# Priority for the emptying of banks in the pairs of the first matrix, and a pinned first step of each pair's weights

## The chip, the cores and the metric

The kernel runs on one core of one Trainium2 chip. The metric is the device time of one execution in microseconds (us); lower is better. Five engines work side by side, each through its own instructions in a fixed order: TensorE (PE in the rows, with its weight loads as PEld), VectorE (DVE), ScalarE (ACT), GpSimd (POOL) and SyncE (SP). The last two issue nearly all transfers here.

## The reference, cut to what matters

The model is a decoder trunk of two layers on 512 tokens of 1024 features in float32. Each layer has a mixer and then a feed-forward part, and it is the second that the change touches:

```
def sqrelu_mlp(x, w1, w2):
    return jnp.square(jax.nn.relu(x @ w1)) @ w2

x = layer_norm(DEEPNORM_ALPHA * x + sqrelu_mlp(x, ffn_w1[l], ffn_w2[l]), ...)
```

`ffn_w1` is 1024 x 4096 and `ffn_w2` is 4096 x 1024.

## The kernel before

Every float32 product is made from split operands. `split` (lines 116 to 118) rounds a tile to a high part on ScalarE (line 117) and subtracts it from the tile on VectorE to get the low part (line 118); three matmuls (high by high, high by low, low by high) then make one product. A weight arrives from HBM as a `raw` tile of 128 x 1024, over SyncE's queue; there are four such buffers, and the next load into one waits until the last step that reads it is done.

The feed-forward part of a layer works through the 4096 hidden features in four blocks of 1024. In each block the first matrix gives the hidden block `hb`, and `second` multiplies it with the second matrix. The hidden features of a block are eight units of 128; the first block does six of them plainly, and all other units are done two at a time by `pair`, with Strassen's scheme in Winograd's form: seven products instead of eight. So there are 13 pairs in a layer: one in block 0 and four in each of blocks 1, 2 and 3.

A pair has three PSUM banks, `ba`, `bb` and `bc`. Its seven products, twelve matmuls each, come in this order: b11 into `ba`; t1 into `bc`; t2 on top of b11 in `ba`; b21 into `bb`; t3 on top in `ba`; b22 on top in `bc`; t4 on top in `ba`. Between them the banks are read out: `p1` is copied from `ba` before t2 adds to it, `p5` from `bc` before b22, `u2` from `ba` before t3 (ScalarE, lines 903, 907 and 911); `c11`, `c22` and `c12` are added up on VectorE (line 826) after b21, t3 and b22. The add of `c22` reads `ba`, and so t4, which writes `ba` again, waits for it. After t4 come a ReLU of `c11` and `c12` together (line 925), of `c22` (927), of `c21` from `ba` (928) and two squares (839). In the last block each square is followed by splits into `hs` and `ho`.

The weights of a pair come from two raw tiles in five steps (`add_pair`): `first` splits one tile (for b11 and b21), `s1` adds the halves of the other tile and splits the sum (t1), `s2` (t2), `s3` (t3 and t4) and `s4` (b22) subtract and split. The steps of a pair are issued while the pair before it runs. In `second`, seven products of 24 matmuls each (line 955) follow; the first uses `o11`, a split of `hb` (`left`).

What sets the order is a scheduler: it takes the program's text, reckons with costs of its own when an instruction can run, and writes one fixed order for each engine. `urgent` runs a function with a raised priority (an offset of 300), so that its instructions, once they can run in the scheduler's reckoning, go ahead of others that stand earlier in the text. `tc.keep_in_program_order(i)` keeps an instruction behind everything that the text has above it on its engine.

Of the kernel before, what the change touches and what calls it, by code (L numbers as in the profile page):

```python
# [11 lines left out]
F32 = mybir.dt.float32  # L12
# [3 lines left out]
AF = mybir.ActivationFunctionType  # L16
ALU = mybir.AluOpType
# [30 lines left out]
def trunk(ctx, tc, a, out):  # L48
    nc = tc.nc
    V, A, G, PE = nc.vector, nc.scalar, nc.gpsimd, nc.tensor  # L50
# [9 lines left out]
    def bank(name="ps"):  # L60
        return psp.tile([P, 512], F32, tag="ps", name=name)
# [17 lines left out]
    def t2(name, shape=(P, 512), dt=F32):  # L79
        return pool["t"].tile(list(shape), dt, tag="t", name=name)  # L80
# [26 lines left out]
    got, ops, held = {}, deque(), deque()  # L107
# [7 lines left out]

    def split(h, l, src):
        A.activation(h, src, AF.Copy)  # L117
        V.tensor_tensor(l, src, h.bitcast(F32), op=ALU.subtract)  # L118

    def room(kind):  # L120
        n = 1 if kind == 1 else 2
# [15 lines left out]
    def ready():  # L137
        need, kind, fn = entries[W["ready"]]
        load_to(need)
        W["ready"] += 1  # L140
        c, h, l = take(kind)
        fn(h, l)
        ops.append((c, h, l))
        load_to(need + W["ahead"])
# [6 lines left out]
    def nxt():  # L151
        if not ops:
            ready()
        c, h, l = ops.popleft()
        held.append(c)
        return c, h, l

    def release(c):
        held.remove(c)
        W[c[0]] -= c[1]  # L160
# [6 lines left out]
    def add_load(dst, src):  # L167

        loads.append(lambda: nc.sync.dma_start(dst(), src))
        return len(loads)  # L170

    def raw(key):
        def dst():
            got[key] = rp.tile([P, 1024], F32, tag="raw", name="raw")
            return got[key]
        return dst
# [6 lines left out]
    def add_pair(u):  # L183

        add_load(raw(u), wst[u])
        k, st = add_load(raw(u + 1), wst[u + 1]), {}
        sub = lambda o, p, q: V.tensor_tensor(o, p, q, op=ALU.subtract)

        def first(h, l):
            split(h, l, got[u])  # L190

        def s1(h, l):
            a2, st["s"] = got[u + 1], t2("s")
            V.tensor_tensor(st["s"], a2[:, :512], a2[:, 512:], op=ALU.add)  # L194
            split(h, l, st["s"])

        def s2(h, l):
            sub(st["s"], st["s"], got[u][:, :512])
            split(h, l, st["s"])

        def s3(h, l):
            a1, a2 = got[u], got.pop(u + 1)
            sub(a2[:, :512], a1[:, :512], a2[:, :512])
            split(h, l, a2)

        def s4(h, l):
            a12 = got.pop(u)[:, 512:]
            sub(a12, a12, st.pop("s"))
            split(h, l, a12)

        return [(k, 2, first), (k, 1, s1), (k, 1, s2), (k, 2, s3), (k, 1, s4)]
# [83 lines left out]
    def urgent(fn):  # L295
        def go(*args, **kw):
            with tc.high_priority(offset=URGENT):
                return fn(*args, **kw)
        return go

    class Fill:
# [3 lines left out]
        def add(self, cost, fn):  # L305
            self.q.append((cost, fn))
# [516 lines left out]
    def ffn(layer, last, nfirst, c0, t_last):  # L823
        new_stage(u=8, h=7, t=4, p=6)
        W["un"] = 1
        add = lambda o, p, q: V.tensor_tensor(o, p, q, op=ALU.add)  # L826
        sub = lambda o, p, q: V.tensor_tensor(o, p, q, op=ALU.subtract)
        H, st = [None, None], {}
# [8 lines left out]
        def square(j, p):  # L837
            r = H[j][:, :, p, :]
            A.activation(r, r, AF.Square)
            if st["fin"]:  # L840
                for i in range(2):
                    h, l = st["hl"][j][i]
                    split(h[:, p, :], l[:, p, :], r[:, i, :])
# [39 lines left out]
        def pair(p, right):  # L883

            ba, bb, bc = (bank("pp")[:, :256] for _ in range(3))

            def prod(o, op, i, r, first):
                for k in range(4):
                    c = slice(512 * i + P * k, 512 * i + P * k + P)
                    w, z = (op[1][:, c], op[2][:, c]), right[r](k)  # L890
                    for n, (x_, y_) in enumerate(((0, 0), (0, 1), (1, 0))):
                        PE.matmul(o, w[x_], z[y_], start=first and k == n == 0, stop=k == 3 and n == 2,  # L892
                                  skip_group_check=True)

            def done(op):
                release(op[0])
                pump(2)

            p1, p5, u2 = t1("p1"), t1("p5"), t1("u2")
            c11, c12, c21, c22 = H[0][:, 0, p, :], H[0][:, 1, p, :], H[1][:, 0, p, :], H[1][:, 1, p, :]  # L900
            w = nxt()
            prod(ba, w, 0, "b11", True)
            A.activation(p1, ba, AF.Copy)
            v = nxt()
            prod(bc, v, 0, "t1", True)
            done(v)
            A.activation(p5, bc, AF.Copy)
            v = nxt()
            prod(ba, v, 0, "t2", False)
            done(v)  # L910
            A.activation(u2, ba, AF.Copy)
            prod(bb, w, 1, "b21", True)
            done(w)
            add(c11, p1, bb)
            w = nxt()
            prod(ba, w, 0, "t3", False)
            add(c22, p5, ba)
            v = nxt()
            prod(bc, v, 0, "b22", False)
            done(v)  # L920
            add(c12, u2, bc)
            prod(ba, w, 1, "t4", False)
            done(w)
            r = H[0][:, :, p, :]
            A.activation(r, r, AF.Relu)
            square(0, p)
            A.activation(c22, c22, AF.Relu)
            A.activation(c21, ba, AF.Relu)
            square(1, p)

        seen = set()

# [5 lines left out]
        def second():  # L938


            c = {k: [bank("pf") for _ in range(2)] for k in "AC"}
            a11, a21, a12, a22 = H[0][:, 0], H[0][:, 1], H[1][:, 0], H[1][:, 1]

            def left(src, halves=False):
                h, l = (t4("ho", (P, 4, 256), F32R) for _ in range(2))
                for z in ((slice(0, 2), slice(2, 4)) if halves else (slice(0, 4),)):
                    split(h[:, z], l[:, z], src[:, z])
                return h, l

            def one(k, op, w, half, tt, first):  # L950
                r = [z.rearrange("p (j c) -> p j c", j=2) for z in w[1:]]
                for j in range(2):
                    l = [z[:, 2 * half + j, tt * P:(tt + 1) * P] for z in op]
                    for n, (x_, y_) in enumerate(((0, 0), (0, 1), (1, 0))):
                        PE.matmul(c[k][tt], l[x_], r[y_][:, j, :], start=first and half == j == n == 0,  # L955
                                  stop=half == j == 1 and n == 2, skip_group_check=True)

            def prod(k, op, first, by_tokens=False):
                if by_tokens:
                    w = [nxt() for _ in range(2)]  # L960
                    for tt in range(2):
                        for half in range(2):
                            one(k, op, w[half], half, tt, first)
                            if tt == 1:
                                release(w[half][0])
                                pump(2)
                    return
                for half in range(2):
                    w = nxt()
                    for tt in range(2):  # L970
                        one(k, op, w, half, tt, first)
                    release(w[0])
                    pump(2)

            o11 = left(a11, True)
            s = t4("s", (P, 4, 256))
            sub(s, a22, a21)
            o1 = left(s)
            prod("A", o11, True)
            into_x(0, 0, c["A"])  # L980
            o12 = left(a12)
            V.scalar_tensor_tensor(s, s, -1.0, a11, op0=ALU.mult, op1=ALU.subtract)
            prod("C", o1, True)
            into_x(1, 1, c["C"])
            V.scalar_tensor_tensor(a12, a12, -1.0, s, op0=ALU.mult, op1=ALU.subtract)
            o2 = left(s)
            c["B"] = [bank("pf") for _ in range(2)]
            prod("B", o12, True)
            into_x(0, 0, c["B"])
            o4 = left(a12)  # L990
            sub(a21, a11, a21)
            prod("A", o2, False)
            into_x(0, 1, c["A"])
            o3 = left(a21)
            prod("C", o4, False)
            into_x(0, 1, c["C"])
            o22 = left(a22)
            prod("A", o3, False, True)
            into_x(1, 1, c["A"])
            prod("A", o22, False, True)  # L1000
            into_x(1, 0, c["A"])
# [423 lines left out]
```

## Time and profile before

| | before |
|---|---|
| time, median of 3 runs | 1175.33 us (1173.59 to 1176.17) |
| time of the profiled execution | 1176.95 us |
| its span, first to last instruction | 1175.2 us |
| busy share of the span: PE, PEld, DVE, ACT, POOL | 97%, 84%, 74%, 53%, 10% |
| mean granted clock of TensorE | 0.99 |

The profiled execution is one run of its own, 1.62 us above the median; 1.75 us of its time lie outside the span. The engine that is busy nearly all the time is TensorE, so what a change can take from the time is mostly in the gaps of that engine and in the stretches in which its clock is lower.

### The profile page before, as it was taken

Reading aid. Unit: us, or ns where it says so; the run is one execution under the profiler, and the core shown is the slowest. Engines: PE = TensorE matmul, PEld = TensorE weight load, DVE = VectorE, ACT = ScalarE, POOL = GpSimd, SP = SyncE. Lnnn points to the kernel's source line nnn. Section 1 sums busy time; section 2 is a strip of 40 time slices with the busy share of each in tenths; the row PEclk is TensorE's granted clock in tenths of the full one; section 3 lists DMA queues with packets and bytes.
Section 4 is the critical chain, followed back from the end, with each engine's and each line's share of the span. In section 5 each row is a group of like instructions: output and inputs, shape, how many; then the busy total and the mean of one; then the engine's idle time right before and its main releaser. Section 6 shows DMA issues by size and latency. Waiting matters only on the chain.

```text
span 1175.2 us, 16786 instructions
## 1 busy us (share of the span) xinstructions
PE 1140.5 (97%) x6538; PEld 988.6 (84%) x6538; DVE 867.2 (74%) x1359; ACT 622.5 (53%) x1046; POOL 119.5 (10%) x148
## 2 busy tenths in 40 slices
PE   8999999999999999999999999999999899999997
PEld 6787787888899798899888888888988888988986
DVE  6677864479895996995657765587879769779846
ACT  6545456536556656565346433543375565664731
POOL 1123310010110110001010000000101001010000
PEclk9999999999999999999999999999999899999999
DMA  7612233072874684535232223410847756654331
GB/s 265 212 54 72 63 123 103 1 196 64 224 192 131 180 215 142 146 108 191 73 104 72 72 72 108 126 54 10 224 123 182 196 145 166 193 167 115 114 107 72
DMA packets 44463, 152.08 MB, mean 129 GB/s; under 512 B 5344, under 2 KB 6368, under 8 KB 44384
## 3 DMA queue, kind: packets, MB, share of 16 engines
q1 hardware_dynamic: 30640, 101.92, 26.3%
q0 software_dynamic: 13744, 49.09, 17.9%
q8 instruction: 51, 0.84, 0.3%
q14 instruction: 28, 0.23, 0.1%
HBM read 142.61 MB, written 2.10 MB: 123 GB/s over the span
## 4 chain that ended last, share of the span: by engine, by line
PE 80%; DVE 6%; ACT 5%; issue 4%; DMA 3%; POOL 1%; DVEq 0%; ACTq 0%; POOLq 0%
PE pf L955 18%; PE pp L892 18%; PE pf L291 4%; PE pf L290 4%; PE pf L292 4%; PE pb L290 4%; PE pb L291 4%; PE pb L292 4%; PE pa L290 3%; DMA raw<-in_wst 3%; PE pa L291 3%; PE pa L292 3%; DVE w L118 2%; ACT w L117 2%; PE pl L1223 1%
## 5 line engine op out<-in xcount | busy, mean ns | idle before, releaser
L118 DVE TENSOR_TENSOR w<-raw,w 128x1024 fp32r<-128x1024 f32 (+2 forms) x210 | 242.4, 1165 | 114.5 <-ACT w L117 91.2
L117 ACT ACTIVATE w<-raw 128x1024 fp32r<-128x1024 f32 (+2 forms) x210 | 205.3, 986 | 159.5 <-issue 26.7
L955 PE MATMUL pf<-w,ho 128*128 128x512 f32 x1008 | 234.6, 391 | 4.9 <-ACT ho L117 4.0
L955 PEld LDWEIGHTS pf<-w,ho 128*128 128x128 f32 x1008 | 187.4, 188 | 48.1 <-ACT ho L117 6.6
L892 PE MATMUL pp<-xTh,w 128*128 128x256 f32 x832 | 159.8, 285 | 0.0
L892 PEld LDWEIGHTS pp<-xTh,w 128*128 128x128 f32 x832 | 134.7, 194 | 0.5
L892 PE MATMUL pp<-T,w 128*128 128x256 f32 x936 | 126.3, 289 | 8.8 <-DVE hb L826 8.8
L892 PEld LDWEIGHTS pp<-T,w 128*128 128x128 f32 x936 | 118.7, 195 | 11.1 <-DVE hb L826 9.6
L892 PE MATMUL pp<-xTl,w 128*128 128x256 f32 x416 | 118.4, 285 | 0.0
L290 PE MATMUL pa<-xTh,w 128*128 128x512 f32 x264 | 106.7, 405 | 0.0
L292 PE MATMUL pa<-xTh,w 128*128 128x512 f32 x264 | 103.6, 392 | 0.0
L291 PE MATMUL pa<-xTl,w 128*128 128x512 f32 x264 | 103.5, 392 | 0.0
L892 PEld LDWEIGHTS pp<-xTl,w 128*128 128x128 f32 x416 | 80.6, 194 | 0.5
L290 PE MATMUL pb<-w,xTh 128*128 128x512 f32 x192 | 76.2, 400 | 1.0 <-ACT w L117 1.0
L291 PE MATMUL pb<-w,xTh 128*128 128x512 f32 x192 | 75.2, 391 | 0.4 <-DVE w L118 0.4
L292 PE MATMUL pb<-w,xTl 128*128 128x512 f32 x192 | 75.2, 392 | 0.0
L117 ACT ACTIVATE w<-ws 128x1024 fp32r<-128x1024 f32 x48 | 50.9, 1060 | 37.0 <-PE pf L955 36.4
L118 DVE TENSOR_TENSOR w<-ws,w 128x1024 fp32r<-128x1024 f32 x48 | 58.1, 1221 | 13.6 <-ACT w L117 8.8
L292 PEld LDWEIGHTS pa<-xTh,w 128*128 128x128 f32 x264 | 50.0, 189 | 10.8
L233 POOL DMA_DIRECT2D ws<-in_wst x24 | 15.1, 632 | 429.3 <-DVE w L118 192.5
L117 ACT ACTIVATE w<-s 128x512 fp32r<-128x512 f32 x52 | 32.6, 628 | 48.8 <-DVE s L194 27.9
L291 PEld LDWEIGHTS pa<-xTl,w 128*128 128x128 f32 x264 | 50.2, 190 | 9.3
(281 smaller groups left out, 2136.5 us busy)
## 6 DMA issues: line engine op xcount, KB each, us to landing
raw<-in_wst SPq DMA_DIRECT2D x178, 512.0 KB, 3.8
ws<-in_wst POOLq DMA_DIRECT2D x72, 512.0 KB, 6.7
ws<-ws POOLq DMA_DIRECT2D x12, 512.0 KB, 5.8
xraw<-in_xT SPq DMA_DIRECT2D x8, 256.0 KB, 4.8
x<-in_x SPq DMA_DIRECT2D x4, 512.0 KB, 6.6
gb<-in_lng POOLq DMA_DIRECT2D x4, 512.0 KB, 5.7
gb<-in_lnb POOLq DMA_DIRECT2D x4, 512.0 KB, 6.8
out_x<-x SPq DMA_DIRECT2D x7, 256.0 KB, 2.0
```

The source lines that it names most:

```text
L117: A.activation(h, src, AF.Copy)
L118: V.tensor_tensor(l, src, h.bitcast(F32), op=ALU.subtract)
L233: tc.keep_in_program_order(nc.gpsimd.dma_start(t, src))
L290: PE.matmul(o, l[0], r[0], start=first, stop=False)
L291: PE.matmul(o, l[0], r[1], start=False, stop=False)
L292: PE.matmul(o, l[1], r[0], start=False, stop=last)
L892: PE.matmul(o, w[x_], z[y_], start=first and k == n == 0, stop=k == 3 and n == 2, skip_group_check=True)
L955: PE.matmul(c[k][tt], l[x_], r[y_][:, j, :], start=first and half == j == n == 0, stop=half == j == 1 and n == 2, skip_group_check=True)
L1223: PE.matmul(pl[:, h * P:(h + 1) * P], z, z, start=True, stop=True)
```

## The change

Two things are done. The copies, adds, ReLUs and squares of `pair`, and the first split `o11` of `second`, are issued with `urgent`; the ReLU and square of `c11` and `c12` move in the text from behind t4 to the place ahead of it. And in `add_pair` two instructions on VectorE are pinned with `keep_in_program_order`: the low half of `first` and the add of `s1`.

```
     def split(h, l, src):
         A.activation(h, src, AF.Copy)
-        V.tensor_tensor(l, src, h.bitcast(F32), op=ALU.subtract)
+        return V.tensor_tensor(l, src, h.bitcast(F32), op=ALU.subtract)
...
         def first(h, l):
-            split(h, l, got[u])
+            tc.keep_in_program_order(split(h, l, got[u]))
...
-            V.tensor_tensor(st["s"], a2[:, :512], a2[:, 512:], op=ALU.add)
+            tc.keep_in_program_order(V.tensor_tensor(st["s"], a2[:, :512], a2[:, 512:], op=ALU.add))
             split(h, l, st["s"])
...
+            r0 = H[0][:, :, p, :]
+            copy, plus = urgent(A.activation), urgent(add)
             w = nxt()
             prod(ba, w, 0, "b11", True)
-            A.activation(p1, ba, AF.Copy)
+            copy(p1, ba, AF.Copy)
...
-            A.activation(p5, bc, AF.Copy)
+            copy(p5, bc, AF.Copy)
...
-            A.activation(u2, ba, AF.Copy)
+            copy(u2, ba, AF.Copy)
...
-            add(c11, p1, bb)
+            plus(c11, p1, bb)
             w = nxt()
             prod(ba, w, 0, "t3", False)
-            add(c22, p5, ba)
+            plus(c22, p5, ba)
             v = nxt()
             prod(bc, v, 0, "b22", False)
             done(v)
-            add(c12, u2, bc)
+            plus(c12, u2, bc)
+            copy(r0, r0, AF.Relu)
+            urgent(square)(0, p)
             prod(ba, w, 1, "t4", False)
             done(w)
-            r = H[0][:, :, p, :]
-            A.activation(r, r, AF.Relu)
-            square(0, p)
-            A.activation(c22, c22, AF.Relu)
-            A.activation(c21, ba, AF.Relu)
-            square(1, p)
+            copy(c22, c22, AF.Relu)
+            copy(c21, ba, AF.Relu)
+            urgent(square)(1, p)
...
-            o11 = left(a11, True)
+            o11 = urgent(left)(a11, True)
```

No instruction is added or removed; the same ones stand in another order. The orders of SyncE and GpSimd do not change at all. In the rows of after, the urgent copies and ReLUs carry line 298, that of the wrapper.

**VectorE, the second pair of block 1 of the first layer.** `raw_3042` and `raw_3044` hold the weights of the third pair (its steps write `w_3255` to `w_3338`), `raw_3123` and `raw_3125` those of the fourth; the three adds that read `p1_3275`, `p5_3276` and `u2_3277` are `c11`, `c22` and `c12` of the second pair. Before:

```order
L118 TENSOR_TENSOR w_3255<-raw_3042,w_3255 128x1024
L194 TENSOR_TENSOR s_3390<-raw_3125 128x512
L118 TENSOR_TENSOR w_3303<-s_3263,w_3303 128x512
L187 TENSOR_TENSOR raw_3042<-raw_3042,s_3263 128x512
L187 TENSOR_TENSOR raw_3125<-raw_3123,raw_3125 128x512
L118 TENSOR_TENSOR w_3334<-raw_3044,w_3333 128x1024
L118 TENSOR_TENSOR w_3338<-raw_3042,w_3338 128x512
L826 TENSOR_TENSOR hb_3134<-p1_3275,pp_3273 128x256
L826 TENSOR_TENSOR hb_3135<-p5_3276,pp_3272 128x256
L826 TENSOR_TENSOR hb_3134<-u2_3277,pp_3274 128x256
```

and after:

```order
L118 TENSOR_TENSOR w_3257<-raw_3042,w_3257 128x1024
L194 TENSOR_TENSOR s_3265<-raw_3044 128x512
L187 TENSOR_TENSOR raw_3044<-raw_3042,raw_3044 128x512
L118 TENSOR_TENSOR w_3264<-s_3265,w_3264 128x512
L187 TENSOR_TENSOR s_3265<-s_3265,raw_3042 128x512
L826 TENSOR_TENSOR hb_3134<-p1_3275,pp_3273 128x256
L187 TENSOR_TENSOR raw_3042<-raw_3042,s_3265 128x512
L118 TENSOR_TENSOR w_3303<-s_3265,w_3303 128x512
L826 TENSOR_TENSOR hb_3135<-p5_3276,pp_3272 128x256
L118 TENSOR_TENSOR w_3334<-raw_3044,w_3333 128x1024
L826 TENSOR_TENSOR hb_3134<-u2_3277,pp_3274 128x256
L118 TENSOR_TENSOR w_3338<-raw_3042,w_3338 128x512
```

Before, the `s1` of the fourth pair (`s_3390`, from `raw_3125`) stands ahead of all three adds; after, nothing of the fourth pair does, and the adds stand among the third pair's steps.

**ScalarE, the end of block 1 of the first layer.** `u2_3523` belongs to the last pair; `ho_3646` is the high part of `o11`, with which `second` begins; `raw_3385` to `raw_3389` and `ws_3136` hold weights of the second matrix. Before:

```order
L911 ACTIVATE u2_3523<-pp_3518 128x256
L117 ACTIVATE w_3581<-ws_3136 128x1024
L117 ACTIVATE w_3613<-ws_3136 128x1024
L927 ACTIVATE hb_3135<-hb_3135 128x256
L117 ACTIVATE w_3632<-raw_3385 128x1024
L925 ACTIVATE hb_3134<-hb_3134 128x2x256
L928 ACTIVATE hb_3135<-pp_3518 128x256
L839 ACTIVATE hb_3134<-hb_3134 128x2x256
L839 ACTIVATE hb_3135<-hb_3135 128x2x256
L117 ACTIVATE ho_3646<-hb_3134 128x512
```

and after:

```order
L298 ACTIVATE u2_3523<-pp_3518 128x256
L117 ACTIVATE w_3581<-ws_3136 128x1024
L117 ACTIVATE w_3613<-ws_3136 128x1024
L298 ACTIVATE hb_3135<-hb_3135 128x256
L298 ACTIVATE hb_3134<-hb_3134 128x2x256
L839 ACTIVATE hb_3134<-hb_3134 128x2x256
L298 ACTIVATE hb_3135<-pp_3518 128x256
L117 ACTIVATE ho_3646<-hb_3134 128x512
L839 ACTIVATE hb_3135<-hb_3135 128x2x256
L117 ACTIVATE w_3634<-raw_3387 128x1024
```

The weight half of 128 x 1024 that stood ahead of the ReLUs now stands behind `o11`, and the second square does too.

**ScalarE, from the third to the fourth pair of the last block of the first layer.** `pp_5034` is bank `ba` of the third pair; `p1_5164`, `p5_5165` and `u2_5166` are the copies of the fourth. Before:

```order
L925 ACTIVATE hb_4752<-hb_4752 128x2x256
L117 ACTIVATE w_5143<-raw_4878 128x1024
L839 ACTIVATE hb_4752<-hb_4752 128x2x256
L928 ACTIVATE hb_4753<-pp_5034 128x256
L117 ACTIVATE hs_4754<-hb_4752 128x256 x2
L839 ACTIVATE hb_4753<-hb_4753 128x2x256
L903 ACTIVATE p1_5164<-pp_5161 128x256
L117 ACTIVATE ho_4756<-hb_4753 128x256
L117 ACTIVATE ho_4758<-hb_4753 128x256
L907 ACTIVATE p5_5165<-pp_5163 128x256
L911 ACTIVATE u2_5166<-pp_5161 128x256
```

and after:

```order
L298 ACTIVATE hb_4752<-hb_4752 128x2x256
L298 ACTIVATE hb_4753<-pp_5034 128x256
L839 ACTIVATE hb_4752<-hb_4752 128x2x256
L839 ACTIVATE hb_4753<-hb_4753 128x2x256
L117 ACTIVATE hs_4754<-hb_4752 128x256 x2
L117 ACTIVATE ho_4756<-hb_4753 128x256
L117 ACTIVATE ho_4758<-hb_4753 128x256
L298 ACTIVATE p1_5164<-pp_5161 128x256
L298 ACTIVATE p5_5165<-pp_5163 128x256
L117 ACTIVATE w_5095<-raw_4748 128x1024
L117 ACTIVATE w_5149<-raw_4884 128x1024
L298 ACTIVATE u2_5166<-pp_5161 128x256
```

The copy `p1` of the next pair now stands behind both squares and all four halves `hs` and `ho`, and two weight halves of 128 x 1024 have come between `p5` and `u2`.

## Rows read from the trace of the kernel before

**Rows 1.** The page: busy us, share of span, instructions of each engine
```profile
PE 1140.5 (97%) x6538; PEld 988.6 (84%) x6538; DVE 867.2 (74%) x1359; ACT 622.5 (53%) x1046; POOL 119.5 (10%) x148
```

**Rows 2.** Waits of PE: engine, line, waited for: us total, times, longest
```profile
PE pp L892 <- DVE hb L826: 8.8, 4, 3.6
PE pf L955 <- ACT ho L117: 4.0, 6, 0.8
...
PE pf L955 <- DVE ho L118: 0.6, 4, 0.2
```

**Rows 3.** Timeline of DVE, 354 to 361: start us, us, what, [idle before <-releaser]
```profile
355.43 0.69 DVE L194 TENSOR_TENSOR s<-raw 128x512 f32<-128x512 f32 x1 [2.49 <-DMA raw<-in_wst]
...
357.84 1.82 DVE L118 TENSOR_TENSOR w<-raw,w 128x1024 fp32r<-128x1024 f32 x2
359.58 0.75 DVE L826 TENSOR_TENSOR hb<-p,pp 128x256 f32<-128x256 f32 x2
```

**Rows 4.** Timeline of PE, 358 to 361
```profile
360.38 0.84 PE L892 MATMUL pp<-T,w 128*128 128x256 f32 x3 [1.87 <-DVE hb L826]
```

**Rows 5.** Chain that ended last, longest pieces: start us, us, what
```profile
290.01 10.07 PE pp L892 x83
...
347.85 7.55 DMA raw<-in_wst
...
360.38 23.48 PE pp L892 x180
...
431.56 6.51 DMA raw<-in_wst
...
443.04 22.01 PE pp L892 x179
...
920.94 9.28 DMA raw<-in_wst
...
935.20 24.46 PE pp L892 x180
...
1007.49 8.03 DMA raw<-in_wst
```

**Rows 6.** Windows: busy us of each engine, granted clock, DMA share, GB/s
```profile
352.00:354.00 2.00, 2.00 (x19) 2.00 (x18) 0.94 (x1) 1.65 (x4) 0.00 (x0) 1.00 1.06 262
...
362.00:364.00 2.00, 2.00 (x11) 2.00 (x10) 0.96 (x1) 1.06 (x3) 0.00 (x0) 0.50 0.57 234
937.00:939.00 2.00, 2.00 (x12) 2.00 (x11) 0.98 (x1) 0.90 (x3) 0.00 (x0) 0.50 0.54 219
1018.00:1020.00 2.00, 0.01 (x1) 0.00 (x0) 2.00 (x4) 0.00 (x0) 0.00 (x0) 1.00 0.01 2
```

**Rows 7.** Timeline, 297 to 306, the end of block 0
```profile
299.99 0.41 DVE L826 TENSOR_TENSOR hb<-u,pp 128x256 f32<-128x256 f32 x1
...
300.11 1.06 ACT L117 ACTIVATE w<-raw 128x1024 fp32r<-128x1024 f32 x1 [1.89 <-PE pp L892]
301.08 0.61 ACT L925 ACTIVATE hb<-hb 128x512 f32<-128x512 f32 x1
...
301.60 0.37 ACT L928 ACTIVATE hb<-pp 128x256 f32<-128x256 f32 x1
301.86 1.14 ACT L839 ACTIVATE hb<-hb 128x512 f32<-128x512 f32 x2
...
302.90 0.62 ACT L117 ACTIVATE ho<-hb 128x512 fp32r<-128x512 f32 x1
...
303.57 1.19 PE L955 MATMUL pf<-w,ho 128*128 128x512 f32 x4 [0.63 <-ACT ho L117]
```

**Rows 8.** Timeline of ACT, 534 to 542, in the last block
```profile
537.35 0.71 ACT L117 ACTIVATE hs<-hb 128x256 fp32r<-128x256 f32 x2
...
538.48 0.37 ACT L903 ACTIVATE p<-pp 128x256 f32<-128x256 f32 x1
538.75 0.71 ACT L117 ACTIVATE ho<-hb 128x256 fp32r<-128x256 f32 x2
```

**Rows 9.** DMA issues: tile, queue, operation xcount, KB each, median us to landing
```profile
raw<-in_wst SPq DMA_DIRECT2D x178, 512.0 KB, 3.8
```

## The prediction

> **What bounds the kernel now.** The page comes first: TensorE is busy for 1140.5 us, 97% of the span, VectorE for 74%, ScalarE for 53% [rows 1]. TensorE's work is untouched here, so the change can only act on what keeps it from running. Its waits come next. In the feed-forward parts two kinds stand out: t4 waits for the add of `c22` four times, 8.8 us in all and 3.6 at the longest, and the first matmuls of `second` wait for the halves of `o11`, 4.0 us for the high one and 0.6 for the low one; the six high waits, three block ends in each of two layers, are never over 0.8 [rows 2]. Third, why `c22` is late. VectorE stands idle for 2.49 us with the add of `s1` of the fourth pair, released by a raw load; behind it come four more steps on weights, and only at 359.58 the adds on the banks [rows 3]. TensorE resumes at 360.38, after 1.87 us [rows 4]. The bank had been full and the add could have run: it stood behind a load that it has nothing to do with.
>
> The Trainium skill (PSUM — Partial Sum Buffer, Engine vs sequencer instructions) says that the queues of ScalarE and VectorE are strict first in, first out. These rows agree: a wait at the head held all that stood behind it. The same rule speaks against the change in the third rival below.
>
> That load took 7.55 us and the three like it in the chain 6.51, 9.28 and 8.03 [rows 5]; while it ran, all sixteen transfer engines were busy (share 1.06) at 262 GB/s [rows 6]. They are the loads at which GpSimd's transfers run beside SyncE's. The change leaves both queues as they are, so I expect them to stay slow.
>
> The waits have an echo. After two of the four the granted clock is 0.50, the lower of TensorE's two levels; in the fourth gap, which fills the window 1018 to 1020, it is still 1.00 [rows 6]. The pieces of the chain behind the first three gaps price it: 179 matmuls at the full clock take 22.01, so 180 take 22.13, against 23.48 and 24.46: 1.35 + 2.33 = 3.7 us [rows 5].
>
> **The change, part by part.** A group of twelve matmuls takes 12 x 10.07 / 83 = 1.46 us and a pair of seven groups 10.19 [rows 5].
>
> *The pins and the urgent adds.* After, `s1` of pair n+2 no longer stands ahead of pair n's adds; these stand among the steps of pair n+1, whose tiles came a pair earlier. What can delay `c22` now is one 512 subtract (0.69, by the add of the same shape) or one split of 512 or 1024 (0.61 or 1.21, the 1.82 shared out by size) [rows 3]. Between t3, after which `c22` may run, and t4 lies b22, 1.46 us; 1.21 + 0.37 for the add is 1.58. So the worst case is 0.1 late, and the four waits fall to nothing or nearly: **8.8**, and with them the **3.7** of the clock. Where does the stall go? `s1` now waits for its load behind the adds; its sum is due a whole pair later, 10.19 us, and a load 2.49 late [rows 3] is still some 4 us early by my chain of the second pair (with the raw buffers freed 1.4 to 1.8 us later than before, since the steps of a pair spread between the adds). SyncE's next load starts as much later; at nothing, with that margin as its cover, which in the second layer is 2 to 3 us.
>
> *The block ends.* Before, ScalarE put a weight half of 1.06 ahead of the ReLU of `c11` and `c12`, and both squares ahead of `ho`, which starts at 302.90; TensorE waited 0.63 for it, from 302.94 to 303.57 [rows 7]. After, the ReLU can follow the add of `c12`, whose 0.41 end at 300.40, and one square (half of 1.14) and the ReLU of `c21` (0.37) follow. By the spacing of the starts before (0.52 after that ReLU, 0.26 after the other, 0.52 a square) `ho` starts near 301.7 and ends at 302.3, ahead of 302.94; its low half, 0.61, ends at 302.9 and is used after the first matmuls, four of which take 1.19 [rows 7]. So these waits go too: 4.0 + 0.6 = **4.6**. The second square and the weight half move behind `o11`, under a first product of 24 matmuls; four for 1.19 make that 7.1 us [rows 7].
>
> In all 8.8 + 3.7 + 4.6 = 17.1 us can be won.
>
> *What is lost.* Copies are urgent only once the scheduler reckons that they can run, so at some places a long instruction now stands ahead of a short one. Below 0 these costs cannot fall. I went through the order on both engines with the durations above:
> - Block 0, one pair: `u2` comes behind two halves of 512 (0.61 to 0.63 each), two of 1024 (1.06 each) and `p5` (0.37), some 3.8 to 4.6, against three groups, 4.37: up to 0.3.
> - Block 1: second pair 0.2 (`p1` and `u2` behind one half), third 0.5 (`c22` behind both splits of `s3` and `s4`, 1.82), fourth 0.3 (`p1` behind the ReLU of `c21` and two squares, 0.37 + 1.14): 1.0.
> - Block 2, fourth pair: `c22` behind a split of a weight of the second matrix, whose high half is itself late on ScalarE: 0.5.
> - Last block: `p1` of the next pair now stands behind the ReLU of `c21` (0.37), both squares (1.14), `hs` (0.71) and `ho` (0.71); with its own 0.37 that is 3.30 from the end of t4 [rows 7, 8]. Until t2 wants it, b11 and t1 run, 2.91, and two matmuls of b21 that are pulled ahead, 0.24: 0.15 late, up to 0.8 if the ReLU ahead of them (0.61) is late too. `u2` behind two halves of 1.06 just passes, 2 x 1.06 + 0.37 = 2.49 against 2.67. I take 1.0 for the block.
>
> That is 2.8 a layer and **5.6** in all. The low bound is 0. For the high one I double it, about 11, since the chains are by hand and an error in one wait repeats in both layers.
>
> Sum: 17.1 - 5.6 = 11.5. The profiled execution of before took 1176.95 us and is 1.6 above the median of 1175.33, so 1165.5 becomes **1164** against the median. Below 0.2% (2.35 us) a measurement of this kernel can't be told from no change.
>
> **The rivals.**
> 1. *All of it, no new stall.* The scheduler's early copies start when the hand chain says and the long instructions ahead of them are idle-time fill, as ScalarE's 53% allows [rows 1]. 1175.3 - 17.1 = 1158. Against it: 3.30 against 3.15 in the last block.
> 2. *More given back.* Raw buffers that come free 1.4 to 1.8 us later move loads into the stretches at share 1.06 [rows 6], where one takes 6.5 to 9.3 us instead of the median 3.8 [rows 5, 9]. If they then land late at two of the four places, 2 x 1.9 (the first wait, [rows 4]) come on top of the 5.6, or the new stalls reach 11: 1168 to 1171.
> 3. *Slower.* An add that is put at the head of VectorE's queue before TensorE has filled its bank holds back the weight steps behind it, and those feed the next pair. VectorE's work per pair is two splits of 1.21, three of 0.61, four sums or differences of 0.69 and three adds of 0.37: 8.1 of 10.2 us, and in the last block, with the low halves of `hs` and `ho`, nearly all of it. So about 2 us of such idling are free in a pair; each us beyond is paid in each of the 24 pairs of blocks 1 to 3. It decides from 17.1 / 24 = 0.7 us over; at 1 us over the time is 1175.3 - 17.1 + 24 = 1182. For it speaks that before, too, the queue was held 2.49 by one head [rows 3]; against it that the adds stand near the middle of their pair's time, with the groups b21, t3 and b22 between them, 1.46 each.
> 4. *It does nothing.* Adds still wait, behind the halves of pair n+1 instead, whose high halves on ScalarE sit behind urgent copies: the same 8.8 in smaller pieces. 1175. Against it: a step that waits for a load is no longer among what is ahead.
>
> The Trainium skill's first page (Trainium Kernel Development and Optimization, Key Constraints) says that transfers of all queues share the same sixteen engines and interleave. The 7.55 us beside the median of 3.8 agree, and by it the second rival is the likeliest way for the loads to spoil part of the gain.
>
> **How the numbers follow.** The sum as it stands, 1160 to 1167: 0.66. In full, about 1158: 0.10. More given back, 1167 to 1171: 0.12. Nothing, 1173 to 1177: 0.05. Slower, 1178 and more: 0.07. The range 1158 to 1171 leaves out the last two and half of what lies under the first rival, under 0.2. The first three cases are faster; with a little of the third taken for a near miss and of the fourth for its other side: faster 0.85, same 0.07, slower 0.08.
>
> **What the profile after would show.** Right: no row of t4 waiting for `hb` above 1 us in all; no stretch at clock 0.50 around 362 and 937; waits of the first matmuls of `second` under 1 us together; on VectorE, an idle time with `s1` still there, released by a raw load, but behind the adds; TensorE's waits for copies, a new row under line 298, of about 5 us, most in the last block and the fourth pair of block 2. Wrong: raw loads named as what TensorE's weights waited for (second rival); idle time of VectorE ahead of line 826, released by TensorE, of over 2 us in a pair, with waits of TensorE for `w` of line 118 (third); the 8.8 still there under other names (fourth). The prediction fails most easily in the 5.6, which rests on chains that no row of before shows, and in the clock, whose fall after two gaps of four the rows show but do not explain.

## The result, and the profile after

| | before | changed |
|---|---|---|
| time, median of 4 runs each | 1175.75 us (1173.59 to 1176.62) | 1159.45 us (1157.03 to 1160.96) |
| ratio to before, 95% interval | | 0.9862 [0.9838, 0.9886] |
| profiled execution, span | 1176.95, 1175.2 us | 1160.96, 1159.2 us |

The changed kernel is faster by 16.3 us. Its time lies 4.55 us under the 1164 that was forecast, inside the range (1158 to 1171) and just outside the forecast's own span for the likeliest case, 1160 to 1167.

The page of the changed kernel, busy us and share of the span:

```profile
PE 1134.2 (98%) x6538; PEld 984.4 (85%) x6538; DVE 869.2 (75%) x1359; ACT 622.6 (54%) x1046; POOL 119.5 (10%) x148
```

Against [rows 1] TensorE moves most: it is 6.3 us less busy for the same matmuls. Of this 3.9 us are the pairs' matmuls, where the stretches of lower clock are gone; most of the rest lies ahead of the first pair, which no edit touches. Its waits, us in all, times, longest:

```profile
PE pf L956 <- DVE ho L118: 1.9, 2, 0.9
PE pf L956 <- DVE x L414: 1.8, 3, 1.2
...
PE pf L956 <- DVE x L416: 0.9, 1, 0.9
```

The two kinds of [rows 2] that mattered are gone: no t4 waits for an add, and no first product of `second` waits for the high half of `o11`. In their place `second` has waits of 4.6 us for sums into `x` and for a low half of `ho`.

The place of [rows 3], VectorE in the second pair of block 1:

```profile
354.54 0.42 DVE L826 TENSOR_TENSOR hb<-p,pp 128x256 f32<-128x256 f32 x1
...
356.08 0.41 DVE L826 TENSOR_TENSOR hb<-p,pp 128x256 f32<-128x256 f32 x1
356.41 1.22 DVE L118 TENSOR_TENSOR w<-raw,w 128x1024 fp32r<-128x1024 f32 x1
357.54 0.41 DVE L826 TENSOR_TENSOR hb<-u,pp 128x256 f32<-128x256 f32 x1
...
359.61 0.68 DVE L194 TENSOR_TENSOR s<-raw 128x512 f32<-128x512 f32 x1
```

and TensorE there, to be held against [rows 4]:

```profile
356.83 1.60 PE L892 MATMUL pp<-T,w 128*128 128x256 f32 x12
358.27 0.28 PE L892 MATMUL pp<-xTh,w 128*128 128x256 f32 x1
```

The add of `c22` ends at 356.49, t4 starts at 356.83 without a wait, and `s1` of the fourth pair, now last, finds its load landed: no idle time stands before it. Twelve matmuls take 1.44 us from start to start.

The end of block 0, as in [rows 7]:

```profile
298.83 0.63 ACT L839 ACTIVATE hb<-hb 128x512 f32<-128x512 f32 x1
298.95 5.86 PE L956 MATMUL pf<-w,ho 128*128 128x512 f32 x25
299.37 0.36 ACT L298 ACTIVATE hb<-pp 128x256 f32<-128x256 f32 x1
299.64 0.62 ACT L117 ACTIVATE ho<-hb 128x512 fp32r<-128x512 f32 x1
```

`ho` comes out one square earlier and TensorE runs on past its first 25 matmuls, where this view ends, while before it stopped after twelve.

Where the time went is best seen in how late TensorE's matmuls start. Where nothing stops it they start 0.12 us apart with 256 columns (1.44 / 12 above) and 0.229 with 512. The table adds up, over the feed-forward parts, every start that comes over 0.05 us behind this pace. It holds waits, what a pause costs beyond the wait that a row shows, and slow stretches of the clock. Each entry comes from one profiled execution, all times are in us, and the last column is the time from the first pair to the end.

| kernel | late in pairs | late in `second` | first pair to end |
|---|---|---|---|
| before | 16.2 | 8.4 | 885.3 |
| changed | 1.6 | 8.5 | 870.4 |
| e1, pin on `s1` alone | 4.4 | 8.9 | 873.5 |
| e2, both pins | 5.4 | 11.8 | 877.7 |
| e3, priority alone | 15.9 | 6.8 | 883.8 |
| e4, smaller GpSimd loads | 1.5 | 0.4 | 862.6 |
| e5 and e11, no pin on `first` | 1.9, 2.0 | 2.1, 5.9 | 864.6, 868.9 |
| e6, `second` urgent | 2.1 | 2.2 | 865.2 |
| e7 and e12, both edits | 1.7, 2.0 | 3.2, 0.5 | 865.3, 863.1 |
| e8, plain squares | 1.1 | 3.5 | 865.2 |
| e9, late `p1` | 2.6 | 10.1 | 873.7 |
| e10, changed kernel again | 1.6 | 3.9 | 866.1 |

So of the 14.9 us between the two profiles from the first pair on, the pairs give 14.6. `second` gives nothing on balance: by this pace the six block ends had cost 6.8 us before, and about as much was lost again later in `second`, most of it in the second layer near 892 and 975.

The larger of these losses, in block 0 of the second layer. ScalarE:

```profile
884.87 1.06 ACT L117 ACTIVATE w<-ws 128x1024 fp32r<-128x1024 f32 x1 [3.34 <-DMA ws<-in_wst]
888.90 1.06 ACT L117 ACTIVATE w<-ws 128x1024 fp32r<-128x1024 f32 x1 [2.97 <-DMA ws<-in_wst]
889.87 1.04 ACT L117 ACTIVATE ho<-hb 128x1024 fp32r<-128x1024 f32 x1
```

VectorE:

```profile
890.00 1.23 DVE L118 TENSOR_TENSOR w<-ws,w 128x1024 fp32r<-128x1024 f32 x1 [2.56 <-ACT w L117]
891.14 1.28 DVE L416 SCALAR_TENSOR_TENSOR x<-x,pf 128x512 f32<-128x512 f32 x2
892.33 1.22 DVE L118 TENSOR_TENSOR ho<-hb,ho 128x1024 fp32r<-128x1024 f32 x1
```

TensorE, and the windows behind it (busy us of PE, PEld, DVE, ACT, POOL, then granted clock, DMA share, GB/s):

```profile
891.97 0.70 PE L956 MATMUL pf<-w,ho 128*128 128x512 f32 x2 [0.92 <-DVE x L416]
893.61 1.65 PE L956 MATMUL pf<-w,ho 128*128 128x512 f32 x3 [0.94 <-DVE ho L118]
```

```profile
894.00:896.00 2.00, 2.00 (x6) 1.52 (x6) 2.00 (x3) 0.39 (x1) 1.09 (x2) 0.50 0.30 49
937.00:939.00 2.00, 2.00 (x19) 2.00 (x19) 0.58 (x1) 1.99 (x4) 0.00 (x0) 1.00 0.66 201
```

It is the mechanism of [rows 3] over again: a weight half waits at the head of ScalarE's queue for a transfer, its low half waits on VectorE, and behind the two stand a sum into `x` and a split of `hb` that could have run. Around 937, where the granted clock was 0.50 before [rows 6], it is now 1.00; instead it falls to 0.50 here.

### The profile page after: what moved, and what is told of

Its sections match the earlier page's. It is cut to its first block, busy times and chain, and to the rows that moved or that the text cites. A ratio compares the mean times of both kernels' runs of the same rounds, so it can differ in the third digit from the quotient of the medians.

```text
span 1159.2 us, 16713 instructions
## 1 busy us (share of the span) xinstructions
PE 1134.2 (98%) x6538; PEld 984.4 (85%) x6538; DVE 869.2 (75%) x1359; ACT 622.6 (54%) x1046; POOL 119.5 (10%) x148
## 4 chain that ended last, share of the span: by engine, by line
PE 74%; DMA 7%; issue 7%; DVE 5%; ACT 4%; POOL 2%; DVEq 0%; POOLq 0%; ACTq 0%
PE pp L892 20%; DMA ws<-in_wst 7%; PE pf L956 7%; PE pa L290 4%; PE pa L292 4%; PE pa L291 4%; PE pf L291 4%; PE pf L290 4%; PE pf L292 4%; PE pb L290 4%; PE pb L291 4%; PE pb L292 4%; PE pl L1224 2%; DVE w L118 2%; ACT w L117 1%
## 5 line engine op out<-in xcount | busy, mean ns | idle before, releaser
L892 PE MATMUL pp<-T,w 128*128 128x256 f32 x936 | 123.4, 284 | 0.0
```

## The experiments

Times are medians, each with its ratio to runs of the kernel before on the same chip.

**e1, the pin on `s1` alone.**

```
 # the kernel before
-            V.tensor_tensor(st["s"], a2[:, :512], a2[:, 512:], op=ALU.add)
+            tc.keep_in_program_order(V.tensor_tensor(st["s"], a2[:, :512], a2[:, 512:], op=ALU.add))
```

> The kernel before with one edit: the add of s1 is pinned, nothing else. Theory (the waits of t4 came from the step of the pair after next at the head of VectorE's queue): this pin alone takes away the four waits of t4 for the adds, 8.8 us, and the stretches at clock 0.50 behind two of them, 3.7 to 3.9; the waits at the block ends stay (4 to 5 us). Time 1175.5 - 12.6 = 1163, ratio 0.989. Rival (it is the priority of the adds that counts): without it adds still stand behind the halves of the next pair, the waits of t4 stay above 5 us, 1170 or more.

1164.43 us, 0.9899 [0.9878, 0.9920]. TensorE's waits in the feed-forward parts:

```profile
PE pf L955 <- ACT ho L117: 4.5, 6, 0.9
...
PE pf L955 <- DVE ho L118: 0.3, 2, 0.2
```

As the theory has it. One line is worth 11.8 us from the first pair on (885.3 - 873.5), all of it in the pairs.

**e2, both pins, no priority.** As e1, and `tc.keep_in_program_order(split(h, l, got[u]))` in `first`.

> The kernel before with both pins and no priority. If the pin on first has work of its own, this is under the run with the pin on s1 alone by over 1 us; my theory gives it nothing, 1163 as well, with the same waits at the block ends.

1165.31 us, 0.9908 [0.9886, 0.9930], no gain over e1; the profile has 2.2 us of waits for sums into `x` that e1 has not.

**e3, priority alone.** The changed kernel without its two `keep_in_program_order`.

> The changed kernel without its two pins: priority and the moved ReLU and square alone. Theory: the waits of t4 for the adds stay near 8.8 us in all, since s1 still stands ahead of the adds in the second pairs, and the six waits for ho at the block ends go: 1175.5 - 5 = 1170.5. Rival (priority is what frees the adds): waits of t4 under 2 us and a time near that of the changed kernel, 1160.

1175.22 us, 0.9998 [0.9977, 1.0020]. The waits, and VectorE ahead of the second of the three:

```profile
PE pp L892 <- DVE hb L826: 8.6, 3, 4.3
...
PE pf L956 <- DVE x L414: 2.0, 2, 1.7
PE pf L956 <- DVE ho L118: 1.5, 2, 0.9
```

```profile
437.45 0.69 DVE L194 TENSOR_TENSOR s<-raw 128x512 f32<-128x512 f32 x1 [3.27 <-DMA raw<-in_wst]
...
441.00 0.74 DVE L826 TENSOR_TENSOR hb<-p,pp 128x256 f32<-128x256 f32 x2
```

The waits of t4 stay (8.6 us against 8.8), since `s1` still stands ahead of the adds. The waits for the high half of `ho` at the block ends go as expected, but the 5 us did not come: `second` has 3.5 us of new waits, and behind those near 988 a stretch at clock 0.50, so that it is 6.8 us late in all. Priority without the pin gives nothing that can be measured.

**e4, smaller transfers.** The changed kernel with half of the columns in two kinds of GpSimd's transfers.

```
         def third(t, half):
-            bring(t, quad(u, 0, 1, half))
-            add_quad(t, quad(u, 1, 1, half))
+            bring(t[:, :512], quad(u, 0, 1, half)[:, :512])
+            add_quad(t[:, :512], quad(u, 1, 1, half)[:, :512])
```

> The changed kernel, in which two transfers of GpSimd per block half (the third sum of the second matrix) bring half of their columns, so that part of that sum is left out. Theory on the new waits of the changed kernel in second (for the sums into x and a late low half, 4.7 us, with a stretch of lower clock behind those near 891, 1 to 1.5 us): they come from these transfers, which land 3.5 us later than before because SyncE's raw loads now run beside them. Then the waits go and the time is 5 to 6 us under the changed kernel, 1153 to 1155. Rival (VectorE has simply too much to do there): the waits stay within 1 us of 4.7, the time 1159.

It leaves out a part of the second matrix's sum, so it shows a cause and is no version to use. 1153.35 us (1151.51 to 1154.22), 0.9801 [0.9774, 0.9827], every run under the fastest of the changed kernel. The waits of `second` are gone, 0.4 us late in all, though VectorE and ScalarE have the same instructions. So they do come from these transfers.

**e5 and e11, no pin on `first`; e10, the changed kernel again.**

```
 # the changed kernel
-            tc.keep_in_program_order(split(h, l, got[u]))
+            split(h, l, got[u])
```

> The changed kernel with the pin on s1 alone; the pin on first is taken out. Theory (the late transfers of GpSimd come from raw buffers that are freed later, which in block 0 is the work of the pin on first): the waits of second near 891 and the stretch of lower clock behind them go, those near 973, a block without a change of that kind, may stay: 1159.5 - 2 to 4 = 1156 to 1157.5. No waits of t4, none for ho at the ends. Rival (priority alone delays the loads, as in the run with priority only): waits of second stay at 4 to 5 us, 1159.5.

> The changed kernel once more, since the run with plain squares lost most of the waits of second without an edit near them. Theory (these waits depend on when transfers land and so vary from execution to execution): the profile has 1 to 5 us of them, at partly other places; the time is 1157 to 1160. Rival (they belong to the order of instructions alone): 4.7 us at the same places near 333, 891 and 973.

> The kernel without the pin on first once more, beside the changed one on the same chip. If the pin on first costs time, this is 1.5 to 3 us faster than the changed kernel; if not, within 1 us of it.

e5 1158.03 us, 0.9847 [0.9824, 0.9870]; e11 1156.78 us, 0.9846 [0.9820, 0.9871]; e10 1158.34 us, 0.9864 [0.9837, 0.9890]. By the time alone the pin on `first` can't be told from nothing: the medians differ by 1.4 us (e5) and 1.6 us (e11 beside e10), with intervals that overlap. The traces tell more. SyncE's last three loads ahead of `second` in block 0 of the second layer, in the changed kernel and in e5:

```profile
858.13 2.07 SPq L169 DMA_DIRECT2D raw<-in_wst  x3
```

```profile
857.37 2.99 SPq L169 DMA_DIRECT2D raw<-in_wst  x3
```

`second` starts at 863.50 in the one and 865.72 in the other, so the first of the three is issued 5.4 us ahead of it with the pin and 8.4 without. GpSimd's next transfers, with the wait for an earlier one to land, in the changed kernel and in e5:

```profile
868.66 0.87 POOL L236 DMA_DIRECT2D ws<-in_wst  x1 [6.49 <-DMA ws<-in_wst]
...
879.15 2.67 POOL L236 DMA_DIRECT2D ws<-in_wst  x3 [9.06 <-DMA ws<-in_wst]
```

```profile
868.51 0.86 POOL L236 DMA_DIRECT2D ws<-in_wst  x1 [4.89 <-DMA ws<-in_wst]
...
876.67 2.67 POOL L236 DMA_DIRECT2D ws<-in_wst  x3 [6.73 <-DMA ws<-in_wst]
```

With the pin, SyncE's loads come closer to GpSimd's; in these two profiles each of GpSimd's then waits longer for the one before, and the last three are issued 15.7 us after the start of `second` instead of 11.0 (in e10 and e11, 13.9 and 11.9). The waits near 891 are in both profiles of the changed kernel and in neither of the other.

Block 0 of the first layer, near 333, says it more clearly, because all profiles can be used. In e2, which differs from e1 by the pin on `first` alone, TensorE waits there as follows, and in e1 it does not wait:

```profile
PE pf L955 <- DVE x L414: 1.2, 1, 1.2
```

All six profiles with this pin and whole transfers (the changed kernel, e2, e6, e8, e9, e10) have waits of `second` there, 0.4 to 2.3 us; the seven without it (before, e1, e3, e5, e7, e11, e12) have none, and neither has e4, with the pin and smaller transfers. In block 0 of the second layer four of the six have them, not e2 and e6. In the other blocks the waits come and go: those near 975 are missing in e10, and e11 has 2.3 us near 1050 that e5 has not.

**e6, `second` urgent; e7 and e12, both edits.** e6 is the changed kernel with

```
-                resid(2 * i + tt, n, bs[tt], None if (i, n) in seen else ALPHA, op=ALU.subtract if n else ALU.add)
+                urgent(resid)(2 * i + tt, n, bs[tt], None if (i, n) in seen else ALPHA, op=ALU.subtract if n else ALU.add)
...
-            o12 = left(a12)
+            o12 = urgent(left)(a12)
```

and `urgent(left)` for the other five splits as well; e7 and e12 also leave out the pin on `first`.

> The changed kernel with the sums into x and all splits of hb in second urgent as well. Theory (late transfers; the sums and splits only stand behind the halves of weights that wait for them): the waits for x and ho go, and in their place stands at most a short wait for the weight half itself, which was ready some 0.2 us after TensorE wanted it: 1154 to 1156. Rival (the transfer itself is the bound at these places): the same 4.7 us under the name of w, 1159.

> Both edits of the two runs before together: pin on s1 alone, the sums into x and all splits of second urgent. If each takes away its own part, this is the fastest, 1153 to 1155, near the run with half of the transfers left out; if they take away the same waits, it is at the better of the two.

> The kernel with both edits (pin on s1 alone, second urgent as well) once more, beside the two others. If it is the best version, 3 to 6 us under the changed kernel; if only the waits of one profile made it look so, within 1.5 us.

e6 1157.78 us, 0.9842 [0.9819, 0.9865], 2 us short of what was expected and not clear of the changed kernel; e7 1154.20 us, 0.9816 [0.9794, 0.9838]; e12 1154.96 us, 0.9824 [0.9797, 0.9852]. Both times the two edits together are the fastest complete version, 3.4 to 5.3 us under the changed kernel, though the intervals touch or overlap. In e6's profile `second` is 2.2 us late, under either profile of the changed kernel.

**e8, plain squares in the last block; e9, `p1` behind one more instruction.**

```
 # e8, for 0 and for 1
-            urgent(square)(0, p)
+            (square if st["fin"] else urgent(square))(0, p)
 # e9
-            copy(p1, ba, AF.Copy)
+            i = copy(p1, ba, AF.Copy)
+            if st["fin"]:
+                tc.keep_in_program_order(i)
...
             copy(c21, ba, AF.Relu)
+            if st["fin"]:
+                copy(c21, c21, AF.Relu)
```

> The changed kernel, but in the last block the squares and the halves behind them have no priority, so that p1 of the next pair mostly stands ahead of them again. The prediction charged their place ahead of p1 with about 1 us a layer, adding durations; then this is 2 us under the changed kernel. Theory now (in the trace of the changed kernel the instructions of ScalarE start 0.21 to 0.52 us apart and p1 ends 0.08 us ahead of t2, so it costs nothing): the same time within 1 us, no waits for copies in either.

> The changed kernel with one more ReLU of c21 (256 columns, no effect on the values) in each pair of the last block, and p1 of the last block pinned behind all of it. Theory: the margin of p1 there is 0.08 us, and one more instruction takes 0.21 to 0.31 us from start to start; waits of t2 for p1 appear, 0.1 to 0.3 us each in up to three pairs a layer, 0.5 to 2 us in all. Rival (the margin is larger than the rows look): no wait for p1.

e8 1156.94 us, 0.9849 [0.9823, 0.9875]: 2.5 us less than the changed kernel and 1.4 less than e10, the same kernel again, so it can't be told from it. Its pairs are 0.5 us less late, not 2; the rest of the difference lies in `second`, which the edit does not touch and which e10 has as short. e9 1163.60 us, 0.9910 [0.9885, 0.9935], and a miss: no wait for `p1` appears, since the scheduler moved other work around the added instruction. Its pairs are 1.0 us later. In each layer a weight load waits 0.3 us for the low half of a weight, and two wait 0.2 each for `u2` and for an add. So e9 says nothing of the margin of `p1`.

## Why the prediction was right, and where its sizes were off

**The pins and the urgent adds: right, and by one pin alone.** 8.8 + 3.7 was forecast; e1 shows that the pin on `s1` does it alone (11.8 us), and e3 that the adds' priority without it does not. The prediction credited the two together. It also expected VectorE to stand idle for the load still, with `s1` behind the adds. That did not come: the row below is the idle time ahead of `s1` before the change, us in all and times, and the changed kernel has none.

```profile
  DMA raw<-in_wst: 11.4, 4
```

By the time `s1` stands at the head, its load has landed, so the stall is not moved but gone. TensorE's busy time on the pairs' matmuls falls by 3.9 us, beside 3.7 forecast for the clock.

**What is lost: the term that failed most, 5.6 us.** Nearly none of it is there: the pairs are 1.6 us late in all, under e1's 4.4. e5, which differs from e1 by the priority and the moved ReLU and square alone, has 1.9. So these win 2.5 us, once the pin is there, where the prediction charged 5.6. They win it in pauses of 0.05 to 0.2 us. TensorE's own rows of waits do not hold these, but those of its weight loads do in part. In e1, for the copy `p1` (line 903) and for an add:

```profile
PEld pp L892 <- ACT p L903: 1.3, 7, 0.2
...
PEld pp L892 <- DVE hb L826: 0.5, 2, 0.3
```

The changed kernel has no such row, and the sign that was named, about 5 us of waits for copies under line 298, did not appear. What failed is the way of adding, as the last block shows. ScalarE in the changed kernel, and TensorE at t2:

```profile
526.76 0.36 ACT L298 ACTIVATE hb<-pp 128x256 f32<-128x256 f32 x1
527.03 1.14 ACT L839 ACTIVATE hb<-hb 128x512 f32<-128x512 f32 x2
528.07 0.71 ACT L117 ACTIVATE hs<-hb 128x256 fp32r<-128x256 f32 x2
528.68 0.71 ACT L117 ACTIVATE ho<-hb 128x256 fp32r<-128x256 f32 x2
529.30 0.64 ACT L298 ACTIVATE p<-pp 128x256 f32<-128x256 f32 x2
```

```profile
529.74 1.68 PE L892 MATMUL pp<-T,w 128*128 128x256 f32 x12
```

The prediction added durations, 0.37 + 1.14 + 0.71 + 0.71 + 0.37 = 3.30. The starts are closer than the durations: from 526.76 to the start of `p1` pass 2.54, with its own 0.37 2.91. t2 starts at 529.74, on its pace, and only its second matmul comes 0.08 late (1.68 for twelve, against 1.60 elsewhere). [rows 7] had shown the spacing (0.26 after a ReLU of 0.37), and for the block end the prediction used it, but not here. Charged that way, 2.91 against 3.15 leaves nothing. In all, such delays of t2 in the last block come to 0.5 us in the two layers, where 2.0 were charged, and e8 has none of them. The chains of the other blocks were not followed one by one; what is left for them is 1.1 us of lateness.

**The block ends: right at their place, wrong in the balance.** The 4.6 us of waits were won at the six ends (e1 still has 4.8 of them). The second rival named what would eat them, raw buffers that come free later and loads that collide, and looked for it at the four waits of t4. It came in `second`, through GpSimd's transfers: "at nothing, with that margin as its cover" was true of SyncE's loads and overlooked the queue beside them. e4 shows the transfers as the cause; e2 beside e1, and e5, show the pin on `first` as what brings the waits in block 0. The waits in the other blocks vary from execution to execution, and what moves those is left open.

The two sums against the table: pairs forecast -12.5 + 5.6 = -6.9, found -14.6; `second` forecast -4.6, found +0.1. The errors, 7.7 us too little and 4.7 too much, partly cancel; that 1164 came within 5 us owes something to luck. The other 1.0 us between the two profiles lies ahead of the first pair, which no edit touches; the profiles of this study differ there by up to 4.8 us (286.9 to 291.7), so differences of 2 us between single profiles are read from the feed-forward parts alone.

**The other rivals.** *Slower:* VectorE does stand idle with an add that waits for TensorE, but for 5.4 us in all, ten times in the run (the last row below) and 7.9 us, ten times, before; no weight of a pair comes late for it.

```profile
L826 DVE TENSOR_TENSOR hb<-p,pp x52: 410/415/422, 295.2 to 1104.6; 128x256 f32<-128x256 f32 x52
...
  PE pp L892: 5.4, 10
```

These are, of the adds on line 826, the durations in ns, and the idle time of the engine before them by what ended it. *Nothing:* e3 has its time, but not its reason: the adds wait behind `s1` again, not behind the halves of the next pair. *All of it:* its 1158 came nearest, but by another sum.

## What to carry to other kernels

Where an in-order queue holds ready work behind a step that waits for a transfer, move that step; priority for the ready work alone gained nothing here on balance. Add up chains on an engine by the distance between starts, not by durations. When a change frees buffers later or earlier, look at every queue that shares the transfer engines, not only at the one that fills these buffers.

## What the runs showed of the hardware

A wait of TensorE costs more than its row. A matmul of 512 columns lasts 0.39 in its rows and the next starts 0.229 after it, so a pause that begins at the end of a row has lost 0.16 already (0.94 in the row at 893.61, 1.11 against the pace). The clock fell behind the gaps of 0.92 and 0.94 near 892, but not behind those of 1.23 and 0.94 near 975, where the windows show 1.00:

```profile
975.07 0.70 PE L956 MATMUL pf<-w,ho 128*128 128x512 f32 x2 [1.23 <-DVE x L414]
976.71 1.65 PE L956 MATMUL pf<-w,ho 128*128 128x512 f32 x6 [0.94 <-DVE ho L118]
```

```profile
977.00:979.00 2.00, 2.00 (x10) 1.62 (x10) 2.00 (x3) 0.64 (x1) 0.61 (x1) 1.00 0.85 338
```

Before the change, too, it fell behind gaps of 1.87 near 360 and 3.58 near 935, but not behind one of 2.48 near 1020. The length of a gap alone did not decide it.

The Trainium skill (PSUM — Partial Sum Buffer, Engine vs sequencer instructions) has ScalarE and VectorE as strict first in, first out. The trace agrees at the new place too: VectorE is idle for 2.56 us until 890.00 with two sums behind, and TensorE then waits 0.92 for one of them. e6 puts those sums and splits ahead and has no wait there, but its transfers are also less late at this place.
